# A hybrid encoder layer on one core: new order of the mixing's projections and jobs, gates as plain f32 products, W_out begun by halves, outputs transposed on TensorE

## The chip, the cores and the metric

One core of a Trainium2 chip runs the whole layer as one program. Its engines are TensorE (PE; its weight loads stand apart as PEld), VectorE (DVE), ScalarE (ACT), GpSimd (POOL) and SyncE (SP), which issues most transfers. The metric is the device time of one execution in microseconds, the median of several runs. Before: 1907.63 us, the median of 3 runs (1907.08 to 1908.33).

## The reference, cut to what matters

One layer on x of 256 tokens by 2048 features, all f32:

```python
x = x + 0.5 * swiglu(rms_norm(x, norm_ffn1), w1_ffn1, w3_ffn1, w2_ffn1)     # 2048 -> 5632 -> 2048
proj = rms_norm(x, norm_mix) @ w_in                                       # q 1024 | k 256 | v 256 | u 1024 | y 1024
q = apply_rope(rms_norm(q, q_norm), cos, sin); k = apply_rope(rms_norm(k, k_norm), cos, sin)
attn_out = bidir_gqa(q, k, v)                                             # 8 heads of 128, 2 for k and v
uc = centred_dw_conv(u, conv_w, conv_b)                                   # width 4
# rglru: r = sigmoid(blocks(uc) @ w_a + b_a); i = sigmoid(blocks(uc) @ w_i + b_i); log_a = -8 * softplus(-lam) * r
#        a = exp(log_a); h_t = a_t * h_(t-1) + sqrt(-expm1(2 * log_a)) * i * uc      (8 blocks of 128)
lru_out = (rglru(uc, ..., False) + rglru(uc, ..., True)) * gelu(y)
x = x + concatenate([attn_out, lru_out]) @ w_out
x = x + 0.5 * swiglu(rms_norm(x, norm_ffn2), w1_ffn2, w3_ffn2, w2_ffn2)
x = x + sigmoid(rms_norm(x, norm_ple) @ w_ple_gate) * (p @ w_ple_proj)
return rms_norm(x, norm_final)
```

## The kernel before, in words

The residual lies transposed in SBUF as `xs`: 128 features on the partitions, 16 blocks of features (`NKD`), 256 tokens. Every large product splits both operands in a rounded high part and a rest (`split`, lines 82 to 84: ACT casts the high part, DVE subtracts for the low part) and adds three products of the fp32r type.

A unit (`unit`, line 131) is one block of 128 output features: 1 MB of weights arrives in a raw buffer (3 of them, on SP's queue), is split in two halves of 8 blocks (4 buffers for each part), and each half gives 8 matmuls of 512 columns (high weights times both parts of the activations) and 8 of 256 (`unit_mms`, line 110). `total` (line 147) adds the two halves of the PSUM tile. The projections of q, k and v (`proj`, line 152) have the tokens on the partitions instead: 4 groups of weights, 24 matmuls of 512 columns each.

Four tiles of PSUM (`acc`) go to units, four (`trp`, tag "tr") to all else. The pool `mid` has 17 buffers of 4 KB per partition, `tok` has 4 of tag "tok", 4 of tag "att" and 6 of tag "tmp".

The mixing runs in this order: eight units of u in two groups, k and v, two groups of q, eight units of y in two groups, sixteen units of W_out. Beside it run jobs (Python generators); `tick` (line 97) advances each by one step, and is called once after each unit and after each group of weights of `proj`. `scan_job` (line 374) splits the convolved u and the gate weights (POOL subtracts), forms the gates with three matmuls each (`mm3`), the decays on ACT (sigmoid, exp, tanh, sqrt) with products on POOL, and runs the recurrence as DVE scans. `q_job` (line 527) does the attention of four heads; `y_job` (line 559) the gelu and its product with the sum of the scans. `rotate` (line 452) applies the rotary table with a scratch tile of tag "att", which the attention's `pt` and `pT_sb` use too. Each engine takes its instructions in one fixed order; a planner writes it when the program is built, by the order of writing as priority and by durations that it simulates.

The head (`lead`, line 251) begins three units with x and weights in pieces; the first pieces of x and the parameters go on ACT's queue. The end: the per-layer gate runs as units; the last two blocks of features are done by halves of the tokens (line 651); for each half the square sums are added by matmuls, the power -1/2 runs on POOL, a matmul broadcasts it over the partitions (`spread`, line 223), and `scale_out` (line 635) scales `xs` in place and stores it transposed; the host puts the axes right.

Of the kernel before, what the change touches and what calls it, by code (L numbers as in the profile page):

```python
# [38 lines left out]
WARM = 8  # L39
# [3 lines left out]
EARLY = 3  # L43
# [4 lines left out]
def hymba_layer(ctx, tc, xT, xrow, pT, w1a, w3a, w2a, win, wqkv, lruw, wout, w1b, w3b, w2b,  # L48
# [52 lines left out]

    def load(dst, src, eng=None):
        loads.append((eng or nc.sync).dma_start(dst, src))
# [27 lines left out]
    def unit(aT, srcs, nk, other=None):  # L131
# [12 lines left out]
        tick()  # L144
# [7 lines left out]
    def proj(aT, srcs):  # L152
        ps = [acc.tile([P, C], F32, tag="acc", name="acc") for _ in range(NH)]
        n = len(srcs)
        for g in range(n):
# [14 lines left out]
            tick()  # L170
# [13 lines left out]
    at = 0  # L184
    for n in PIECES[:EARLY]:
        load(flat(xs[:, at:at + n, :]), xT[:, at * S:(at + n) * S], nc.scalar)
        if at == 0:
            load(par_sb, par, nc.scalar)
        at += n
# [22 lines left out]
    def inv_rms(*ssq, halves=range(NH), keep=True):  # L212


        ps = trp.tile([P, 2, S], F32, tag="tr", name="sums")
        n = len(halves)
        for i, h in enumerate(halves):
            for j, s in enumerate(ssq):
                nc.tensor.matmul(ps[:, 0, i:i + 1], lhsT=s[:, h * P:(h + 1) * P], rhs=ones[:, 0:1],
                                 start=j == 0, stop=j == len(ssq) - 1)  # L220
        return spread(ps[:, 0, :n], n, keep)

    def spread(sums, n=NH, keep=True):

        r = sml.tile([P, NH], F32, tag="inv", name="inv", bufs=2)[:, :n]
        rsqrt(r, sums, D, n)
        dg = tmp("dg")
        pb = trp.tile([P, 2, S], F32, tag="tr", name="rows")
        for i in range(n):
            cols = slice(i * P, (i + 1) * P)  # L230
            nc.vector.tensor_scalar(dg[:, cols], ident, r[:, i:i + 1], None, op0=ALU.mult)
            nc.tensor.matmul(pb[:, 0, cols], lhsT=ones, rhs=dg[:, cols], start=True, stop=True)
        if not keep:
            return r, pb[:, 0, :n * P]
# [4 lines left out]
    def add_square(ssq, n, cols=slice(0, S), eng=None):  # L239

        if n == 0:
            nc.scalar.activation(ssq[:, cols], xs[:, n, cols], AF.Square)
            return
        t = tmp("sqr")[:, cols]
        nc.scalar.activation(t, xs[:, n, cols], AF.Square)  # L245
        (eng or nc.gpsimd).tensor_tensor(ssq[:, cols], ssq[:, cols], t, op=ALU.add)  # L246
# [127 lines left out]
    def scan_job(g, u):  # L374
        hi = mid.tile([P, 4, S], F32R, tag="mid", name="uc_hi")
        lo = mid.tile([P, 4, S], F32R, tag="mid", name="uc_lo")
        split(u, hi, lo, nc.gpsimd)
        raw = wraw.tile([P, 4, C], F32, tag="raw", name="raw")
        in_order(nc.sync.dma_start(flat(raw), lruw[g]), loads[-1])
        yield  # L380
        gw = []
        for d in range(2):
            wh = mid.tile([P, 2, C], F32R, tag="mid", name="gw_hi")
            wl = mid.tile([P, 2, C], F32R, tag="mid", name="gw_lo")
            split(raw[:, 2 * d:2 * d + 2, :], wh, wl, nc.gpsimd)
            gw.append((wh, wl))
        yield
        r, i, a = [], [], []
        for d in range(2):
            wh, wl = gw[d]  # L390
            for m in range(2):
                o = mtile("gate")
                for b in range(2):
                    ps = trp.tile([P, 2, S], F32, tag="tr", name="tr")
                    for j in range(2):
                        k = 2 * b + j
                        wc = slice(k * P, (k + 1) * P)
# [7 lines left out]
                yield  # L405
            cb = cneg[:, 8 * d + 4 * g:8 * d + 4 * g + 4].unsqueeze(2).broadcast_to([P, 4, S])
            nc.gpsimd.tensor_tensor(r[d], r[d], cb, op=ALU.mult)
        for d in range(2):
# [4 lines left out]
            nc.gpsimd.tensor_tensor(flat(i[d]), flat(i[d]), flat(u), op=ALU.mult)  # L413
        yield
# [3 lines left out]
        for d in range(2):  # L418
            nc.vector.scalar_tensor_tensor(flat(r[d]), flat(a[d]), 1.0, flat(r[d]),
                                           op0=ALU.add, op1=ALU.mult)  # L420
            nc.gpsimd.tensor_tensor(flat(r[d]), flat(r[d]), flat(i[d]), op=ALU.mult)
# [4 lines left out]
            yield  # L426
        nc.gpsimd.tensor_tensor(flat(i[0]), flat(i[0]), flat(i[1]), op=ALU.add)
# [3 lines left out]
    for g in range(2):  # L431
        u = mtile("uc")
        for k in range(4):
# [3 lines left out]
            nc.gpsimd.tensor_tensor(t, t, rmB, op=ALU.mult)  # L437
# [14 lines left out]
    def rotate(src, nh, half, m):  # L452
# [3 lines left out]
        sq = tok.tile([P, C], F32, tag="att", name="sq", bufs=ATT)[:, :w].rearrange("p (h d) -> p h d", d=HD)  # L456
# [61 lines left out]
    def values(qc, hp, pT2):  # L518
# [5 lines left out]
        dst = mix2[2 * qc + hp]  # L524
# [18 lines left out]
    mix2 = [mid.tile([P, 2, 2, S], F32R, tag="mid", name="mixT") for _ in range(NKD // 2)]  # L543
    mixT = [mix2[k // 2][:, k % 2, :, :] for k in range(NKD)]
# [14 lines left out]
    def y_job(g, y):  # L559
        for b in range(2):  # L560
            part = y[:, 2 * b:2 * b + 2, :]
            nc.scalar.activation(part, part, AF.Gelu_apprx_tanh)
            nc.vector.tensor_tensor(part, part, hsum[g][:, 2 * b:2 * b + 2, :], op=ALU.mult)
            dst = mix2[4 + 2 * g + b]
            split(part, dst[:, :, 0, :], dst[:, :, 1, :])
        yield

    for g in range(2):
        y = mtile("y")
        for k in range(4):  # L570
# [3 lines left out]
            nc.gpsimd.tensor_tensor(y[:, k, :], t, rmB, op=ALU.mult)  # L574
        jobs.append(y_job(g, y))

    tick()
# [184 lines left out]
```

## Time and profile before

| what | before |
|---|---|
| median of 3 runs | 1907.63 us |
| the profiled execution's own time | 1907.39 us |
| its span | 1905.6 us |
| PE busy | 1872.7 us (98%) |
| DVE busy | 1203.6 us (63%) |
| ACT busy | 965.2 us (51%) |
| POOL busy | 292.6 us (15%) |
| HBM read | 349.00 MB, 184 GB/s over the span |
| a load of 1024 KB of W_out, issue to landing (median) | 4.8 us |

A matmul's end is modelled, so a busy PE is not PE at its peak: the granted clock of a stretch says whether it ran at 2.4 GHz (1.00) or partly at 1.2 GHz. An engine's idle time is put down to what ended last before it went on. In the view by windows the busy times stand in the order PE, PEld, DVE, ACT, POOL, each with its count of instructions; in groups by line, the busy us, the mean ns of one and the idle us before them, with what ended it, stand behind the bar.

### The profile page before, as it was taken

What the parts mean: (1) busy time and instruction counts of PE and PEld (TensorE: products, weight loads), DVE (VectorE), ACT (ScalarE), POOL (GpSimd) and SP (SyncE); (2) the same over time, 40 slices, a digit from 0 to 9 for tenths busy, and PEclk for the clock granted to TensorE, in tenths of its full rate; (3) what the DMA queues carried; (4) which work ended last, traced back from release to release, by engine and by line L of the source; (5) the groups of instructions that cost most, each with busy time, mean ns of one, the idle gap of its engine ahead of it and who ended that gap; (6) DMA issues with size and microseconds to landing.
All of it is one profiled execution on the core that took longest, in us unless ns stands there. A gap on an engine that the chain in (4) does not pass through costs nothing.

```text
span 1905.6 us, 27228 instructions
## 1 busy us (share of the span) xinstructions
PE 1872.7 (98%) x10632; PEld 1640.3 (86%) x10632; DVE 1203.6 (63%) x1723; ACT 965.2 (51%) x1494; POOL 292.6 (15%) x225
## 2 busy tenths in 40 slices
PE   9999999999999999988999999999999999999997
PEld 7888888888888888867878888888888888888886
DVE  6766655556566556888767666655555666655686
ACT  6544444444444445677654544444444444555553
POOL 0111100011111001564211111110001111101143
PEclk9999999999999999999999999999999999999998
DMA  8555545655555556544345555555565555555552
GB/s 316 205 189 187 192 160 190 210 199 179 197 180 176 182 184 213 175 152 155 133 152 181 191 185 194 182 186 167 194 208 196 181 195 184 202 197 195 201 177 67
DMA packets 61552, 352.85 MB, mean 185 GB/s; under 512 B 6512, under 2 KB 12144, under 8 KB 31088
## 3 DMA queue, kind: packets, MB, share of 16 engines
q1 hardware_dynamic: 60848, 350.51, 54.0%
q8 instruction: 83, 1.36, 0.3%
q10 hardware_dynamic: 576, 0.61, 0.1%
q14 instruction: 45, 0.37, 0.1%
HBM read 349.00 MB, written 2.10 MB: 184 GB/s over the span
## 4 chain that ended last, share of the span: by engine, by line
PE 92%; DVE 3%; ACT 3%; issue 1%; POOL 1%; DMA 0%; SPq 0%; POOLq 0%; DVEq 0%; ACTq 0%
PE acc L115 59%; PE acc L117 30%; DVE wlo L84 1%; DVE gate L424 1%; DVE uc L370 0%; ACT whi L83 0%; PE po L522 0%; PE acc L656 0%; PE pe L115 0%; POOL us L437 0%; DMA xs<-in_xT 0%; PE tr L495 0%; ACT gate L403 0%; ACT a L410 0%; ACT L416 0%
## 5 line engine op out<-in xcount | busy, mean ns | idle before, releaser
L84 DVE TENSOR_TENSOR wlo<-raw,whi 128x1024 fp32r<-128x1024 f32 x722 | 806.5, 1126 | 594.7 <-ACT whi L83 577.5
L83 ACT CAST whi<-raw 128x1024 fp32r<-128x1024 f32 x722 | 687.0, 952 | 814.5 <-PE acc L115 553.9
L115 PE MATMUL acc<-aT,whi 128*128 128x512 f32 x3296 | 832.0, 393 | 1.2 <-DVE aT L88 1.2
L115 PEld LDWEIGHTS acc<-aT,whi 128*128 128x128 f32 x3296 | 593.1, 189 | 107.8 <-DVE aT L88 2.7
L117 PEld LDWEIGHTS acc<-aT,wlo 128*128 128x128 f32 x3296 | 451.4, 191 | 32.7
L117 PE MATMUL acc<-aT,wlo 128*128 128x256 f32 x3296 | 463.0, 283 | 0.0
L115 PE MATMUL acc<-hT,whi 128*128 128x512 f32 x1408 | 364.8, 392 | 0.0
L304 POOL TENSOR_TENSOR s<-s,rB 128x256 f32<-128x256 f32 x88 | 123.8, 1407 | 1067.7 <-ACT s L301 1061.9
L115 PEld LDWEIGHTS acc<-hT,whi 128*128 128x128 f32 x1408 | 247.6, 189 | 37.2
L117 PEld LDWEIGHTS acc<-hT,wlo 128*128 128x128 f32 x1408 | 202.7, 190 | 21.3
L117 PE MATMUL acc<-hT,wlo 128*128 128x256 f32 x1408 | 209.0, 282 | 0.0
L246 POOL TENSOR_TENSOR ssq<-ssq,sqr 128x256 f32<-128x256 f32 x58 | 54.4, 939 | 339.6 <-ACT sqr L245 339.6
L115 PE MATMUL acc<-mixT,whi 128*128 128x512 f32 x256 | 64.6, 393 | 1.4 <-DVE mixT L84 1.4
L115 PEld LDWEIGHTS acc<-mixT,whi 128*128 128x128 f32 x256 | 45.9, 189 | 10.2 <-DVE mixT L84 2.1
L315 DVE SCALAR_TENSOR_TENSOR xs<-acc,xs 128x256 f32<-128x256 f32 x128 | 53.3, 417 | 0.0
L87 ACT ACTIVATE aT<-xs,par_sb 128x256 fp32r<-128x256 f32 x64 | 31.5, 506 | 41.9 <-DVE xs L315 39.3
L92 PE MATMUL acc<-wlo,aT 128*128 128x512 f32 x96 | 40.4, 421 | 11.3 <-DVE wlo L84 11.3
L88 DVE SCALAR_TENSOR_TENSOR aT<-xs,par_sb,aT 128x256 fp32r<-128x256 f32 x64 | 38.2, 610 | 19.4 <-ACT aT L87 19.1
L306 DVE TENSOR_TENSOR u<-u,s 128x256 f32<-128x256 f32 x88 | 37.4, 426 | 9.1 <-DVE u L149 0.5
L93 PE MATMUL acc<-whi,aT 128*128 128x512 f32 x96 | 39.8, 415 | 0.0
L84 DVE TENSOR_TENSOR hT<-u,hT 128x256 fp32r<-128x256 f32 x88 | 38.0, 431 | 1.9 <-ACT hT L83 1.9
L300 DVE TENSOR_TENSOR z<-z,rB 128x256 f32<-128x256 f32 x88 | 37.4, 425 | 2.7
(168 smaller groups left out, 1001.5 us busy)
## 6 DMA issues: line engine op xcount, KB each, us to landing
raw<-in_w2a SPq DMA_DIRECT2D x64, 704.0 KB, 4.0
raw<-in_w1b SPq DMA_DIRECT2D x44, 1024.0 KB, 4.8
raw<-in_w3b SPq DMA_DIRECT2D x44, 1024.0 KB, 4.9
raw<-in_w2b SPq DMA_DIRECT2D x64, 704.0 KB, 4.0
raw<-in_w3a SPq DMA_DIRECT2D x43, 1024.0 KB, 4.8
raw<-in_w1a SPq DMA_DIRECT2D x42, 1024.0 KB, 4.8
raw<-in_win SPq DMA_DIRECT2D x16, 1024.0 KB, 4.9
raw<-in_wout SPq DMA_DIRECT2D x16, 1024.0 KB, 4.8
```

The source lines that it names most:

```text
L83: nc.scalar.copy(hi, src)
L84: (eng or nc.vector).tensor_tensor(lo, src, f32(hi), op=ALU.subtract)
L88: nc.vector.scalar_tensor_tensor(lo, src, gain, f32(hi), op0=ALU.mult, op1=ALU.subtract)
L92: nc.tensor.matmul(ps, lhsT=ah, rhs=wl, start=False, stop=False)
L93: nc.tensor.matmul(ps, lhsT=al, rhs=wh, start=False, stop=last)
L115: nc.tensor.matmul(ps, lhsT=ws[i][0], rhs=acts[i], start=first and i == 0, stop=False)
L117: nc.tensor.matmul(ps[:, 1, :], lhsT=ws[i][1], rhs=acts[i][:, 0, :], start=False, stop=last and i == n - 1)
L246: (eng or nc.gpsimd).tensor_tensor(ssq[:, cols], ssq[:, cols], t, op=ALU.add)
L300: nc.vector.tensor_tensor(z, z, rB, op=ALU.mult)
L304: nc.gpsimd.tensor_tensor(s, s, rB, op=ALU.mult)
L306: nc.vector.tensor_tensor(u, u, s, op=ALU.mult)
L315: nc.vector.scalar_tensor_tensor(xs[:, n, :], ps[:, j, :], 0.5, xs[:, n, :], op0=ALU.mult, op1=ALU.add)
```

## The change

Four parts.

- Mixing, order: k and v stand between the two groups of u; jobs advance after each half unit (after every second block of `proj`), and `scan_job` and `y_job` have shorter steps. Tiles for the mixed features are taken when they are written. The rows of W_out stand in a new order (`MIX_ORDER`), and its first two units are begun with the half that holds the first four heads and the first group of the recurrence.
- Mixing, work: the gates are one plain f32 matmul each, without splits; elementwise products on POOL go to DVE; `rotate` takes its scratch from tag "tok".
- The head: parameters and the third piece of x on SP's queue, ACT's table load ahead of its second piece, 6 warm-up matmuls for 8.
- The end: the gated features of both halves of the tokens first, then the blocks of `xs` are transposed on PE back to tokens on partitions, scaled from PSUM by a column on ACT or DVE into tiles of their own and stored in the final layout.

```diff
-WARM = 8
+MIX_ORDER = [*range(4), *range(8, 12), *range(4, 8), *range(12, 16)]
+WARM = 6
-EARLY = 3
+EARLY = 2
...
                 unit_mms(ps, part, aT[at:at + len(part)], at == 0, at + len(part) == n)
                 at += len(part)
-        tick()
+                tick()
...
-            tick()
+                if k % 2:
+                    tick()
...
+    load(par_sb, par)
+    load(flat(xs[:, 0:1, :]), xT[:, 0:S], nc.scalar)
     warm = sml.tile([P, 1], F32, tag="warm", name="warm", bufs=1)
     nc.gpsimd.memset(warm, 0.0)
     nc.scalar.activation(warm, warm, AF.Silu)
+    load(flat(xs[:, 1:2, :]), xT[:, S:2 * S], nc.scalar)
...
     def scan_job(g, u):
-        split(u, hi, lo, nc.gpsimd)
...
+            w = mid.tile([P, 2, C], F32, tag="mid", name="gw")
+            load(flat(w), lruw[g, :, 2 * C * d:2 * C * (d + 1)])
...
-                        mm3(ps[:, j, :], wh[:, m, wc], wl[:, m, wc], hi[:, k, :], lo[:, k, :],
-                            True, True)
+                        nc.tensor.matmul(ps[:, j, :], lhsT=gw[d][:, m, k * P:(k + 1) * P], rhs=u[:, k, :],
+                                         start=True, stop=True)
...
-            nc.gpsimd.tensor_tensor(r[d], r[d], cb, op=ALU.mult)
+            nc.vector.tensor_tensor(r[d], r[d], cb, op=ALU.mult)
+            yield
...
-            nc.gpsimd.tensor_tensor(flat(i[d]), flat(i[d]), flat(u), op=ALU.mult)
-        yield
+            nc.vector.tensor_tensor(flat(i[d]), flat(i[d]), flat(u), op=ALU.mult)
+            yield
...
-            nc.gpsimd.tensor_tensor(flat(r[d]), flat(r[d]), flat(i[d]), op=ALU.mult)
+            yield
+            nc.vector.tensor_tensor(flat(r[d]), flat(r[d]), flat(i[d]), op=ALU.mult)
+            yield
...
-        nc.gpsimd.tensor_tensor(flat(i[0]), flat(i[0]), flat(i[1]), op=ALU.add)
+        nc.vector.tensor_tensor(flat(i[0]), flat(i[0]), flat(i[1]), op=ALU.add)
...
-            nc.gpsimd.tensor_tensor(t, t, rmB, op=ALU.mult)
+            nc.vector.tensor_tensor(t, t, rmB, op=ALU.mult)
...
-        sq = tok.tile([P, C], F32, tag="att", name="sq", bufs=ATT)[:, :w].rearrange("p (h d) -> p h d", d=HD)
+        sq = tok.tile([P, C], F32, tag="tok", name="sq")[:, :w].rearrange("p (h d) -> p h d", d=HD)
...
-        nc.gpsimd.tensor_tensor(sv, sv, cb, op=ALU.mult)
+        nc.vector.tensor_tensor(sv, sv, cb, op=ALU.mult)
...
+    u_part(0)
     v_sb = const.tile([P, NH, 2 * HD], F32, name="v_sb")
     pkv = proj(am, [wqkv[2, k] for k in range(4)])
...
+    u_part(1)
     for qc in range(2):
         pq = proj(am, [wqkv[qc, k] for k in range(4)])
...
-            nc.gpsimd.tensor_tensor(y[:, k, :], t, rmB, op=ALU.mult)
-        jobs.append(y_job(g, y))
+            nc.vector.tensor_tensor(y[:, k, :], t, rmB, op=ALU.mult)
+            if k % 2:
+                jobs.append(y_job(g, k // 2, y[:, k - 1:k + 1, :]))
...
+    first = [acc.tile([P, 2, S], F32, tag="acc", name="acc") for _ in range(2)]
+    raws = []
+    for n in range(2):
+        raws.append(wraw.tile([P, 16, P], F32, tag="raw", name="raw"))
+        load(flat(raws[n]), wout[n, 0])
+    for j in (0, 8):
+        if j:
+            finish()
+        for n in range(2):
+            hi, lo = spl_pair()
+            split(raws[n][:, j:j + 8, :], hi, lo)
+            blocks = [mix2[k // 2][:, k % 2, :, :] for k in MIX_ORDER[j:j + 8]]
+            unit_mms(first[n], [(hi[:, i, :], lo[:, i, :]) for i in range(8)], blocks, j == 0, j == 8)
+            tick()
...
+    last_features(0)
+    last_features(1)
+    r0 = norms(0)
+    for b in range(4):
+        put(0, b, in_rows(0, b), r0)
+    ahead = [in_rows(1, b) for b in range(3)]
+    r1 = norms(1)
+    for b in range(3):
+        put(1, b, ahead[b], r1)
+    put(1, 3, in_rows(1, 3), r1)
```

`finish` advances the jobs until none is left. The new functions at the end:

```python
def last_features(h):          # the two last feature blocks for half h of the tokens
    ...
    nc.scalar.activation(last[i][:, cols], x, AF.Square)
    nc.scalar.activation(x, x, AF.Copy, scale=par_at(O_GF + n))
def norms(h):                  # three sum matmuls of one column, then the power on POOL
    ...
    rsqrt(r, ps[:, 0, :1], D, 1)
    return r
def in_rows(h, b):             # four blocks of features back to tokens on partitions
    ...
    for k in range(4):
        nc.tensor.transpose(ps[:, k * P:(k + 1) * P], xs[:, 4 * b + k, h * P:(h + 1) * P], ident)
    return ps
def put(h, b, ps, r):          # b odd: DVE, even: ACT
    if b % 2 == 0:
        outs[h, b // 2] = mid.tile([P, 2, C], F32, tag="mid", name="out")
    o = outs[h, b // 2][:, b % 2, :]
    if b % 2:
        nc.vector.tensor_scalar(o, ps, r, None, op0=ALU.mult)
    else:
        nc.scalar.activation(o, ps, AF.Copy, scale=r)
    eng = nc.scalar if (h, b) == (1, 2) else nc.sync
    eng.dma_start(out[h * P:(h + 1) * P, b * C:(b + 1) * C], o)
```

## Rows read from the trace of the kernel before

**Rows 1.** Windows: us; busy us (count) by engine; granted clock; DMA share; GB/s.

```profile
26.20:740.00 713.80, 713.80 (x4094) 628.32 (x4093) 429.85 (x628) 344.32 (x508) 71.91 (x58) 1.00 0.57 192
...
740.00:965.00 225.00, 207.19 (x1078) 175.64 (x1077) 172.11 (x213) 151.24 (x259) 91.88 (x51) 0.96 0.45 156
...
830.00:853.00 23.00, 17.32 (x58) 12.84 (x58) 22.47 (x23) 14.38 (x29) 13.83 (x8) 0.85 0.26 91
853.00:888.00 35.00, 27.65 (x117) 22.01 (x117) 27.21 (x31) 22.33 (x40) 15.63 (x8) 0.90 0.44 146
...
900.00:951.60 51.60, 51.60 (x299) 45.62 (x298) 37.36 (x62) 33.94 (x64) 9.98 (x9) 1.00 0.43 144
951.60:964.10 12.50, 7.90 (x31) 5.34 (x29) 6.62 (x17) 9.34 (x19) 0.72 (x1) 0.86 0.24 84
```

**Rows 2.** Waits of PE, 746.7 to 1050.8 us: total us, times, longest.

```profile
PE acc L92 <- DVE wlo L84: 11.3, 5, 4.7
```

**Rows 3.** DVE groups by line, 100 to 400 us, then 740 to 965 us.

```profile
L84 DVE TENSOR_TENSOR wlo<-raw,whi 128x1024 fp32r<-128x1024 f32 x96 | 117.6, 1225 | 122.9 <-ACT whi L83 122.8
...
L300 DVE TENSOR_TENSOR z<-z,rB 128x256 f32<-128x256 f32 x16 | 6.8, 426 | 0.5
...
L84 DVE TENSOR_TENSOR wlo<-raw,whi 128x1024 fp32r<-128x1024 f32 x60 | 87.0, 1464 | 23.0 <-ACT whi L83 18.9 <-ACT pT_sb L515 2.0 <-ACT rB L236 1.5
L424 DVE TENSOR_TENSOR_SCAN gate<-a,gate 128x256 f32<-128x256 f32 x16 | 18.3, 1199 | 0.0
```

**Rows 4.** Timeline of DVE and of POOL in the scan: start us, us.

```profile
810.61 9.80 DVE L84 TENSOR_TENSOR wlo<-raw,whi 128x1024 fp32r<-128x1024 f32 x3 [2.12 <-ACT whi L83]
...
832.14 6.74 DVE L424 TENSOR_TENSOR_SCAN gate<-a,gate 128x256 f32<-128x256 f32 x4
...
839.92 2.42 DVE L424 TENSOR_TENSOR_SCAN gate<-a,gate 128x256 f32<-128x256 f32 x4
...
815.94 3.39 POOL L413 TENSOR_TENSOR gate<-gate,uc 128x1024 f32<-128x1024 f32 x1
```

**Rows 5.** Timeline of PE in the mixing.

```profile
793.70 0.28 PE L91 MATMUL tr<-uc_hi,gw_hi 128*128 128x256 f32 x1
...
795.14 0.40 PE L91 MATMUL acc<-whi,aT 128*128 128x512 f32 x1
...
906.88 0.82 PE L513 MATMUL tr<-ident,pt 128*128 128x128 f32 x6
...
911.62 1.89 PE L522 MATMUL po<-pT_sb,v_sb 128*128 128x256 f32 x8
913.35 1.89 PE L495 MATMUL tr<-kT,qT 128*128 128x256 f32 x8
...
959.19 3.49 PE L522 MATMUL po<-pT_sb,v_sb 128*128 128x256 f32 x8 [0.95 <-ACT pT_sb L515]
...
972.62 2.00 PE L115 MATMUL acc<-mixT,whi 128*128 128x512 f32 x8
...
975.41 2.00 PE L115 MATMUL acc<-mixT,whi 128*128 128x512 f32 x8
```

**Rows 6.** Timeline of POOL, the rotation of the second group of q.

```profile
917.09 1.32 POOL L461 TENSOR_TENSOR qs<-qs,tabs 128x512 f32<-128x512 f32 x1 [17.41 <-DVE sq L460]
```

**Rows 7.** Timeline of the end: PE, POOL, DVE and SP's queue.

```profile
1889.99 0.84 PE L656 MATMUL acc<-aT,whi 128*128 128x256 f32 x5
...
1896.73 0.56 POOL L210 TENSOR_TENSOR inv<-rs_v,mhalf 128x1 f32<-128x1 f32 x1 [0.89 <-DVE rs_v L209]
...
1898.56 2.54 DVE L639 TENSOR_TENSOR xs<-xs,rows 128x256 f32<-128x256 f32 x5 [0.95 <-PE rows L232]
...
1899.00 2.93 SPq L641 DMA_DIRECT2D out<-xs  x5
```

**Rows 8.** The chain that ended last, in the head, and ACT's timeline there.

```profile
6.08 5.69 DMA xs<-in_xT
...
11.79 1.31 ACT L87 ACTIVATE aT<-xs,par_sb 128x256 fp32r<-128x256 f32 x3 [1.69 <-DMA xs<-in_xT]
```

More of the change, by code (lines that the diff above doesn't have):

```diff
@@ L100, in tick, with finish @@
                 jobs.remove(job)
+    def finish(done=lambda: not jobs):
+        while not done():
+            tick()
     def load(dst, src, eng=None):
@@ L556, in hymba_layer, with y_job @@
         jobs.append(q_job(qc, qro, qsc))
[L559 to L565, printed above, removed]
+    def y_job(g, b, part):
+        nc.scalar.activation(part, part, AF.Gelu_apprx_tanh)
+        nc.vector.tensor_tensor(part, part, hsum[g][:, 2 * b:2 * b + 2, :], op=ALU.mult)
+        dst = mix2[4 + 2 * g + b] = mixtile()
+        split(part, dst[:, :, 0, :], dst[:, :, 1, :])
         yield
     for g in range(2):
+        finish(lambda: hsum[g] is not None)
         y = mtile("y")
@@ L633, in hymba_layer @@
     last = [sml.tile([P, S], F32, tag=t, name="last", bufs=2) for t in ("ssq", "rB")]
-    def scale_out(h, rows, part, eng):
-        cols = slice(h * P, (h + 1) * P)
-        for at, n in ((0, 2), (2, 2)) if part == 0 else ((4, 4), (8, 4), (12, 4)):
-            o = xs[:, at:at + n, cols]
-            eng.tensor_tensor(o, o, rows.unsqueeze(1).broadcast_to([P, n, P]), op=ALU.mult)
-            b, e = at // 4, at % 4
-            nc.sync.dma_start(out[h, b, :, e:e + n, :], o)
     small = []
@@ L650, in hymba_layer @@
         small.append(t)
-    for h in range(NH):
+    def last_features(h):
         cols = slice(h * P, (h + 1) * P)
+        pss = []
         for i in range(2):
@@ L661, in hymba_layer @@
             nc.vector.tensor_tensor(g, g, rpB[:, cols], op=ALU.mult)
-            gated(n, g, pe[i], cols, nc.vector, last[i])
-        _, rf = inv_rms(ssq3, *last, halves=[h], keep=False)
-        if h == 0:
-            rows = tmp("rows")[:, :P]
-            nc.scalar.copy(rows, rf)
-            scale_out(0, rows, 0, nc.gpsimd)
-        else:
-            scale_out(0, rows, 1, nc.vector)
-            scale_out(1, rf, 0, nc.vector)
-            scale_out(1, rf, 1, nc.vector)
+            x = xs[:, n, cols]
+            nc.scalar.activation(g, g, AF.Sigmoid)
+            nc.vector.tensor_tensor(g, g, pe[i][:, cols], op=ALU.mult)
+            nc.vector.tensor_tensor(x, x, g, op=ALU.add)
+            nc.scalar.activation(last[i][:, cols], x, AF.Square)
+            nc.scalar.activation(x, x, AF.Copy, scale=par_at(O_GF + n))
+    def norms(h):
+        cols = slice(h * P, (h + 1) * P)
+        ps = trp.tile([P, 2, S], F32, tag="tr", name="sums")
+        for j, q in enumerate((ssq3, *last)):
+            nc.tensor.matmul(ps[:, 0, 0:1], lhsT=q[:, cols], rhs=ones[:, 0:1], start=j == 0, stop=j == 2)
+        r = sml.tile([P, NH], F32, tag="inv", name="inv", bufs=2)[:, :1]
+        rsqrt(r, ps[:, 0, :1], D, 1)
+        return r
+    def in_rows(h, b):
+        if b % 2:
+            ps = trp.tile([P, C], F32, tag="tr", name="out")
+        else:
+            ps = acc.tile([P, C], F32, tag="acc", name="out")
+        for k in range(4):
+            nc.tensor.transpose(ps[:, k * P:(k + 1) * P], xs[:, 4 * b + k, h * P:(h + 1) * P], ident)
+        return ps
+    outs = {}
+    def put(h, b, ps, r):
+        if b % 2 == 0:
+            outs[h, b // 2] = mid.tile([P, 2, C], F32, tag="mid", name="out")
+        o = outs[h, b // 2][:, b % 2, :]
+        if b % 2:
+            nc.vector.tensor_scalar(o, ps, r, None, op0=ALU.mult)
+        else:
+            nc.scalar.activation(o, ps, AF.Copy, scale=r)
[11 more added lines that the diff above has]
+    put(1, 3, in_rows(1, 3), r1)
 def _units(w, kc=None):
@@ L759 @@
     r = run_bass_kernel_spmd(nc, [sent], core_ids=[0])
[L760 to L761 removed]
+    return r.results[0]["out_0"].reshape(1, S, D)
```

95 lines of the change are left out of this document (37 added, 58 removed).

## The prediction

> **What bounds the kernel now.** I read the windows first, because TensorE (PE) is the bound and the question is where it is not full. Between 26.2 and 740 us PE is busy for the whole stretch at granted clock 1.00, so no edit outside the mixing, the head and the tail can gain [rows 1]. In the mixing three stretches fall short: 830 to 853 us (17.32 of 23.00 busy, clock 0.85), 853 to 888 us (27.65 of 35.00, 0.90) and 951.6 to 964.1 us (7.90 of 12.50, 0.86). Idle: 5.68 + 7.35 + 4.60 = 17.6 us. Clock, as (1 - granted) times the stretch: 3.45 + 3.50 + 1.75 = 8.7 us. Together 26.3 us can be had back in the mixing, and no more.
>
> Next, the waits of PE: the largest, 11.3 us in 5 pieces, is a matmul of a projection waiting for the low part of a weight split by VectorE (DVE) [rows 2]. So in the first two stretches DVE is late; its window says so too, 22.47 busy of 23.00 [rows 1]. Why is it late? By lines, one 128x1024 split takes 1225 ns on DVE between 100 and 400 us, but 1464 on the mean of 60 in the mixing [rows 3]. The timeline shows when: three splits take 9.80 us from 810.61 while GpSimd (POOL) runs products of the scan, one of them 3.39 us from 815.94; four scans take 6.74 us from 832.14 and the like four 2.42 us, 0.605 each, from 839.92 [rows 4]. Taking every form between 740 and 965 us at its short executions removes 42 us from DVE (an estimate; the splits give 60 x 0.24 = 14 of it, the scans 16 x 0.59 = 9.5). DVE was busy 172 us there [rows 1]; undisturbed it would be 130.
>
> **Part by part. Mixing: work moved.** Seven kinds of products go from POOL to DVE: 14 of 128x1024 (the decay constant 4, input times u 4, the product after the root 4, the sum of both directions 2), 16 of 128x256 for u and y, 4 of 128x512 and 2 of 128x256 in the rotation. At 1.225 and 0.426 us [rows 3], and 0.7 for 128x512 (an estimate between these two), that is 17.2 + 7.7 + 2.8 = 27.7 us. The splits of u (2 of 128x1024) and of the gate weights (4) vanish from POOL, with as many casts on ScalarE (ACT), 6 us off the latter. DVE then has 130 + 28 = 158 us where it had 172, and POOL keeps only small powers.
>
> This rests on the long executions standing only beside POOL [rows 4]; were they caused by something that stays, DVE would have 172 + 28 = 200 us, the first rival. The Trainium skill ("SBUF — State Buffer", Who interferes with whom) gives a mechanism: DVE's second read port is shared with GpSimd under an exclusive lock, so a DVE operation with two SBUF inputs waits out a GpSimd one that reads SBUF. By that rule DVE has the 158 us; the trace agrees with it in the two groups of four scans, 6.74 and 2.42 us.
>
> **Mixing: gates as plain f32 products.** 32 products of two instructions each replace 96 matmuls. Twelve of the old take 1.44 us (793.70 to 795.14), 0.12 each: 11.5 us. Eight f32 instructions of the same size in the values take 1.73 us (911.62 to 913.35), 0.216 each: 64 are 13.8 us [rows 5]. PE pays 2.3 us, in full since it is the bound.
>
> **Mixing: order.** k and v now come between the two groups of u, and jobs advance every half unit. I counted DVE against PE by section at undisturbed durations. Second u group: per unit two splits 2.45, total and product 0.85, three taps 1.3 (estimate from the 0.426), so 18.4 for four; k's norm and rotation 4.1 (an estimate, some 16 small steps); five scan products 6.1; 29 us of DVE in 24 of PE (four units of 5.59 and eight f32 gate instructions). First y group: 13.2 own, 4.9 rotation, 8 attention (estimate: half of the 16 us of its lines now), 8.5 scan (8 x 0.605 + 3 x 1.225), 1.4 gelu; 36 us in 31 of PE (four units and 9 of attention). In the other five sections DVE has slack of 3 to 15 us. Overload: 5 + 5 = 10 us. Four buffers of split weights are four half units of 2.79 us (972.62 to 975.41), 11 us of PE [rows 5], and hide all of it if they are full when the overload starts. If nothing hides it, PE waits 10 us and loses clock in the proportion seen before (8.7 on 17.6): 15 us. I take the middle, 7.5: the stretch from 740 then lasts 208.5 us after the terms below, and DVE is busy 158 of it, 76%, the same share as now (172 of 225), so the forecast asks no better packing of DVE than there is.
>
> **Mixing: rotation and W_out.** Before, the rotation of the second q waits for scratch held by the attention: POOL stands 17.41 us until 917.09 [rows 6], and the last attention job ends PE's third gap. With scratch from the other pool this goes, and the first halves of two output units (2 x 2.79 = 5.6 us) need none of the late tiles. What is late next is the last gelu: seven steps on ACT and DVE of 0.4 to 0.7 us each and perhaps a table load, about the 5.6 us of cover, so 0 to 1 us shows; it is inside the 7.5. Two raw weights held there leave one buffer for the next load, which is issued about 11 us (four half units) ahead of need.
>
> Mixing: 26.3 - 7.5 - 2.3 = 16.5 us gained.
>
> **Tail.** PE's last product before ends at 1890.8, with sums put between; without these about 1890.3 [rows 7]. Before, the power on POOL (0.56 us, at 1896.73), a broadcast and five scalings (2.54 us from 1898.56) follow, and the second half's five issues begin at 1899.00. After: 6 sum matmuls (0.1 us each, an estimate from the 0.12 of the gates), 16 transposes of the first half and 12 of the second, 6 sums, the power and its step on DVE (1.0), then outputs from PSUM in pairs, one on ACT and one on DVE, 0.7 each. Six transposes took 0.82 us at 906.88 [rows 5], so 28 are 3.8. From 1890.3: sums to 1890.9, transposes to 1894.7, sums to 1895.3, power to 1896.3, first output at 1897.0, so the issues begin 2.0 us sooner. The 1 MB behind them then needed the rest of the span, 6.6 us from 1899.0, and still does, since it was issued over 2.93 us and now over little less. The separate output tiles keep a scaling from waiting for a transfer; I cost that at nothing. Bounds: 0 if the first half's scalings get in front of the last sigmoid chain (four of 0.7 us on two engines, and hops), 5 if the sums go ahead of the transposes and the issues shrink to 1 us. I take 2.
>
> **Head.** The parameters and the third piece of x move from ACT's queue to SP's, two issues in front of the later pieces and weights; the table load comes before the second piece; two warm-up matmuls go. PE is fed by the fourth piece of x, for which ACT waits 1.69 us at 11.79; its transfer is 5.69 us of the chain, from the issue at 6.08 [rows 8], so the queue was full of bytes, and the bytes in front are the same. Bounds: -0.5 (first split sooner) to +1.5 (third piece late). I take +0.5.
>
> **Sum.** The profiled execution took 1907.4 (span 1905.6 and 1.8 around it; the median of the runs is 0.2 above). 1907.4 - 16.5 - 2 + 0.5 = 1889.4, say 1889. Its own range: best 26.3 - 2.3 + 5 + 0.5 = 29.5 less, 1878; worst 26.3 - 15 - 2.3 + 0 - 1.5 = 7.5 less, 1900.
>
> **Rivals.**
> 1. The stretching stays. DVE then has 200 us; at an occupancy between its mean (0.765) and its fullest stretch (0.977), 0.87, that is 230 us for what lasts 225: 1907.4 + 5 - 2 + 0.5 = 1911. For it: I infer the cause from overlaps in time. Against: the two groups of four scans, and the splits in the first 700 us, where POOL is seldom busy. Chance 0.05.
> 2. The transposes of the tail run at 1.2 GHz. Eight f32 instructions took 3.49 us at 959.19, in the stretch of clock 0.86, against 1.89 at 911.62 [rows 1, 5], 1.85 times; 28 transposes cost 3.2 us more and the tail loses 1.2: 1892.6. For it: transposes stand alone there for 3 us. Against: PE comes straight from matmuls, and six at 906.88 ran at full speed, though among matmuls. The Trainium skill ("TensorE: Matmul & The Clock Gate", Part 4: PE-mode transpose) says that the full clock does not engage for transposes; no row here shows a stretch of them alone. Chance 0.13.
> 3. The change doesn't do what it says: the planner sets each engine's order by its own simulated times, and could put the late halves of the output units first, so that the third gap (4.60 + 1.75 = 6.3 us) stays: 1895.7. Against: the early halves are written first and need nothing late. Chance 0.08.
> 4. Slower: DVE becomes the bound with holes in it. The scan chain now alternates ACT and DVE on a queue that is taken in order; each hop that the planner mistimes leaves DVE idle with the splits queued behind, and PE behind these. The place is the second u and the first y group. It decides at 158 / 225 = 70% occupancy: below that the mixing is longer than now. Between the 53% of 951.6 to 964.1 and the mean of 76.5% [rows 1] lies 65%: 243 us, 18 more: 1907.4 + 18 - 2 + 0.5 = 1924. For it: both groups are over 100% by count. Against: 900 to 951.6, where DVE and ACT alternate most, had 72% without making PE wait. Chance 0.18.
>
> **Chances.** Forecast 0.56. A measurement of this kernel can tell about 0.2%, 3.8 us: below 1903.8 is faster, above 1911.4 slower. Faster: 0.56 + 0.13 + 0.08 + 0.01 (the lower edge of rival 4), 0.78. Slower: 0.02 of rival 1 and 0.13 of rival 4, 0.15. The same: 0.03 + 0.04, 0.07. The range goes from 1878 to 1908: below it lies 0.03, above 0.03 of rival 1 and 0.14 of rival 4.
>
> **What would show it.** Splits in the mixing near 1225 ns on the mean, and scans near 2.4 us for four: else rival 1. PE idle under 8 us between 746 and 964, with no half clock: else rival 4, and the wait on the low split then stands in the two overloaded sections. No gap before W_out's first full units: else rival 3. Transposes of the tail 0.1 to 0.14 us apart: else rival 2, or the tail's order. The first real matmul by 5 us and no PE gap over 1 us at 12: else the head. Wrong altogether if the gates on PE cost far over 13.8 us, or PE waits for ACT's tables instead.

## The result, and the profile after

The changed kernel takes 1884.24 us (median of 4 runs, 1883.70 to 1884.46), the kernel before 1907.98 (4 runs, 1907.08 to 1908.74): a ratio of 0.9875 with a 95% interval of 0.9858 to 0.9892, or 23.7 us less. Forecast were 1889 us and "faster" at 0.78.

The profiled execution of the changed kernel took 1884.04 us with a span of 1882.2. Four points of the two traces split the difference of the spans, 23.4 us. The mixing runs from the first matmul of its projections to the first one of the second FFN; the tail from the first product for the last two blocks of features to the end of the span.

| stage | before, us | after, us | gained | forecast |
|---|---|---|---|---|
| head and first FFN, to the mixing's start | 746.7 | 749.1 | -2.4 | -0.5 |
| mixing | 304.1 | 282.3 | 21.8 | 16.5 |
| second FFN and gate | 827.9 | 827.9 | 0 | 0 |
| tail | 26.9 | 22.9 | 4.0 | 2 |

The page's first and fourth part, busy time and the shares of the chain that ended last by engine:

```profile
span 1882.2 us, 27165 instructions
...
PE 1868.5 (99%) x10626; PEld 1639.5 (87%) x10626; DVE 1182.6 (63%) x1745; ACT 960.3 (51%) x1496; POOL 209.0 (11%) x181
...
PE 97%; ACT 1%; DVE 1%; DMA 0%; issue 0%; SPq 0%; DVEq 0%; POOLq 0%; POOL 0%; ACTq 0%
```

Windows of the changed kernel: the head, PE's time on the second group of u, the two stretches of the mixing that had been short of PE in [rows 1], PE's time on the first group of y, the stretch that now holds all that is left of its idle time, and two of the end (columns as in [rows 1]):

```profile
0.00:26.20 26.20, 21.61 (x88) 16.26 (x89) 16.14 (x36) 16.79 (x38) 0.92 (x9) 0.93 0.86 307
799.35:824.07 24.72, 24.72 (x142) 21.70 (x141) 19.41 (x35) 18.84 (x35) 2.46 (x2) 1.00 0.52 174
830.00:853.00 23.00, 23.00 (x103) 18.95 (x102) 22.66 (x32) 14.73 (x24) 0.00 (x0) 1.00 0.53 183
853.00:888.00 35.00, 35.00 (x172) 29.66 (x171) 26.03 (x44) 26.91 (x67) 4.82 (x4) 1.00 0.46 153
877.56:909.00 31.44, 31.44 (x183) 27.77 (x182) 27.90 (x48) 29.61 (x55) 2.63 (x2) 1.00 0.35 118
...
900.00:975.00 75.00, 72.43 (x414) 63.11 (x413) 59.02 (x93) 47.80 (x80) 3.79 (x4) 1.00 0.48 164
...
1871.00:1876.40 5.40, 4.63 (x43) 4.43 (x43) 3.28 (x11) 2.86 (x8) 1.12 (x2) 1.00 0.28 105
1876.40:1882.20 5.80, 0.00 (x0) 0.00 (x0) 1.33 (x2) 1.19 (x2) 0.00 (x0) 0.76 0.71 264
```

From 830 to 888 us PE is full at granted clock 1.00, where it had been busy for 17.32 of 23 and 27.65 of 35 us at 0.85 and 0.90. DVE is still busy for 22.66 of 23: it is packed, not freed. All waits of PE in the mixing, 749 to 1031 us (total, times, longest), answer to [rows 2]; the wait on a weight's low part is gone:

```profile
PE acc L123 <- DVE mixT L88: 2.0, 1, 2.0
PE po L522 <- ACT pT_sb L515: 0.4, 1, 0.4
PE tr L513 <- DVE pt L506: 0.2, 1, 0.2
```

DVE by lines in the mixing, splits of a weight and scans, answering to [rows 3] (their means were 1464 and 1199 ns; over the same 740 to 965 us as there, the splits' mean is 1221 ns too):

```profile
L88 DVE TENSOR_TENSOR wlo<-raw,whi 128x1024 fp32r<-128x1024 f32 x89 | 108.4, 1221 | 41.5 <-ACT whi L87 39.6 <-ACT rB L239 1.5
...
L421 DVE TENSOR_TENSOR_SCAN gate<-a,gate 128x256 f32<-128x256 f32 x16 | 9.8, 671 | 0.0
```

DVE's timeline, answering to [rows 4 and 6]: both groups of four scans at the short duration, a rotation's product that was POOL's, and the last two splits that PE waits for:

```profile
835.17 2.43 DVE L421 TENSOR_TENSOR_SCAN gate<-a,gate 128x256 f32<-128x256 f32 x4
...
838.63 2.43 DVE L421 TENSOR_TENSOR_SCAN gate<-a,gate 128x256 f32<-128x256 f32 x4
...
857.32 0.69 DVE L460 TENSOR_TENSOR qs<-qs,tabs 128x512 f32<-128x512 f32 x1
...
943.39 0.69 DVE L88 TENSOR_TENSOR mixT<-po,mixT 128x512 fp32r<-128x512 f32 x1 [3.59 <-ACT mixT L87]
944.00 0.68 DVE L88 TENSOR_TENSOR mixT<-y,mixT 128x512 fp32r<-128x512 f32 x1
```

PE's timeline, answering to [rows 5]: gates in plain f32 and the products after them, a longer stretch of such gates, then the last gap of the mixing:

```profile
798.67 1.02 PE L392 MATMUL tr<-uc,gw 128*128 128x256 f32 x4
799.35 2.20 PE L123 MATMUL acc<-aT,whi 128*128 128x512 f32 x8
801.39 1.11 PE L125 MATMUL acc<-aT,wlo 128*128 128x256 f32 x8
...
849.61 1.89 PE L392 MATMUL tr<-uc,gw 128*128 128x256 f32 x8
...
940.74 1.99 PE L522 MATMUL po<-pT_sb,v_sb 128*128 128x256 f32 x8 [0.40 <-ACT pT_sb L515]
944.74 0.73 PE L123 MATMUL acc<-mixT,whi 128*128 128x512 f32 x2 [2.00 <-DVE mixT L88]
```

ACT's timeline at that gap:

```profile
942.77 0.59 ACT L87 CAST mixT<-po 128x512 fp32r<-128x512 f32 x1 [1.60 <-PE po L522]
943.25 0.62 ACT L87 CAST mixT<-y 128x512 fp32r<-128x512 f32 x1
```

The timeline of all engines at the end, answering to [rows 7], with a few of its lines:

```profile
1871.18 1.18 PE L695 MATMUL out<-ident,xs 128*128 128x128 f32 x9
...
1872.34 2.27 PE L695 MATMUL out<-ident,xs 128*128 128x128 f32 x19
...
1874.06 4.28 SPq L709 DMA_DIRECT2D out<-out  x7
...
1874.50 0.31 ACT L676 ACTIVATE last<-xs 128x128 f32<-128x128 f32 x1
...
1876.32 1.41 DVE L705 TENSOR_SCALAR out<-out,inv 128x512 f32<-128x512 f32 x2 [0.67 <-POOL inv L216]
```

And ACT's and PE's timelines in the head, answering to [rows 8]:

```profile
12.63 1.71 ACT L91 ACTIVATE aT<-xs,par_sb 128x256 fp32r<-128x256 f32 x4 [0.78 <-DMA xs<-in_xT]
```

```profile
13.71 0.50 PE L123 MATMUL acc<-aT,whi 128*128 128x512 f32 x1 [2.49 <-DVE aT L92]
```

### The profile page after: what moved, and what is told of

Its sections match the earlier page's. It is cut to its first block, busy times and chain, and to the rows that moved or that the text cites. A ratio compares the mean times of both kernels' runs of the same rounds, so it can differ in the third digit from the quotient of the medians.

```text
span 1882.2 us, 27165 instructions
## 1 busy us (share of the span) xinstructions
PE 1868.5 (99%) x10626; PEld 1639.5 (87%) x10626; DVE 1182.6 (63%) x1745; ACT 960.3 (51%) x1496; POOL 209.0 (11%) x181
## 4 chain that ended last, share of the span: by engine, by line
PE 97%; ACT 1%; DVE 1%; DMA 0%; issue 0%; SPq 0%; DVEq 0%; POOLq 0%; POOL 0%; ACTq 0%
PE acc L123 60%; PE acc L125 31%; PE acc L97 1%; PE acc L95 1%; PE acc L96 1%; PE tr L392 1%; DMA xs<-in_xT 0%; PE acc L664 0%; PE pe L123 0%; PE po L522 0%; DVE wlo L88 0%; ACT whi L87 0%; PE small L653 0%; PE pe L125 0%; PE tr L495 0%
## 5 line engine op out<-in xcount | busy, mean ns | idle before, releaser
L88 DVE TENSOR_TENSOR wlo<-raw,whi 128x1024 fp32r<-128x1024 f32 x722 | 792.5, 1105 | 597.7 <-ACT whi L87 583.1
L304 ACT ACTIVATE s<-z 128x256 f32<-128x256 f32 x88 | 36.4, 413 | 4.3 <-DVE z L303 4.3
```

What stands on the lines that cost most here:

```text
L88: (eng or nc.vector).tensor_tensor(lo, src, f32(hi), op=ALU.subtract)
L304: silu = nc.scalar.activation(s, z, AF.Silu)
```

## The experiments

"Mixing", "start" and "tail" below are the stages of the table, read from each run's trace in the same way; times are medians of 4 runs (t1: 11; d1: one); the brackets hold the ratio to the kernel before on the same chip and its 95% interval. A trace is of one execution, which need not lie at the median: those of p1 (1890.0 us) and p2 (1894.8) lie 2.9 and 1.9 us below it, those of r1 (1888.8) and k1 (1893.9) 2.3 and 1.5 us above.

**The head of before in the changed kernel** (h1). The edit puts the order and the queues of the first loads and the warm-up count back:

```diff
-WARM = 6
+WARM = 8
-EARLY = 2
+EARLY = 3
-    load(par_sb, par)
-    load(flat(xs[:, 0:1, :]), xT[:, 0:S], nc.scalar)
+    at = 0
+    for n in PIECES[:EARLY]:
+        load(flat(xs[:, at:at + n, :]), xT[:, at * S:(at + n) * S], nc.scalar)
+        if at == 0:
+            load(par_sb, par, nc.scalar)
+        at += n
...
-    load(flat(xs[:, 1:2, :]), xT[:, S:2 * S], nc.scalar)
```

> The changed kernel with the head of before (parameters and third piece of x on ACT's queue, 8 warm-up matmuls). Theory (the new head costs what the first mixing matmul came later, 749.11 against 746.72): 2.4 us less than the changed kernel, about 1881.8, and the mixing starts at 746.7. Rival (the head only shifts with the phase of the clock from run to run): no steady difference, 1884.

1882.93 us (0.9868, 0.9854 to 0.9881); start 747.4, 1.7 us sooner than 749.1 where 2.4 was expected; mixing 282.3, tail 22.9, both unchanged. Its window of the head:

```profile
0.00:26.20 26.20, 22.98 (x100) 16.95 (x101) 16.69 (x37) 17.65 (x38) 0.92 (x9) 1.00 0.88 317
```

The granted clock stays at 1.00, where the changed head has 0.93, a stretch of 3.4 us at the lower level from 15.7 us. PE's wait before the fourth piece of x is 1.48 us here and 2.49 there.

**The products of POOL on DVE, alone in the kernel before** (p1), seven lines of this form:

```diff
-            nc.gpsimd.tensor_tensor(r[d], r[d], cb, op=ALU.mult)
+            nc.vector.tensor_tensor(r[d], r[d], cb, op=ALU.mult)
```

> The kernel before with one part: the seven kinds of products of the mixing on DVE instead of POOL; the splits of u and of the gate weights stay on POOL, order and everything else as before. Theory (POOL beside DVE stretches DVE and makes PE wait): the waits of PE on low splits fall from 11.3 us to under 4, mean split in the mixing under 1.30 us, 10 to 17 us less, 1891 to 1898; the third gap (951.6 to 964.1) stays. Rival (the new order is what helps, and DVE only gets more work): 1905 or above.

1892.87 us (0.9917, 0.9904 to 0.9931). By the medians it is 15.7 us less than before. In the traced execution the mixing takes 286.6 us, 17.5 less than before; splits have a mean of 1244 ns over the mixing (1386 before, over the same stretch); DVE, with all these products added, is busy for 223.9 us of the mixing instead of 228.7. PE's waits there, the longest kinds:

```profile
PE tr L513 <- DVE pt L506: 3.2, 3, 1.9
PE acc L92 <- DVE wlo L84: 2.1, 2, 1.3
```

The wait on the low part of a weight goes from 11.3 us [rows 2] to 2.1 with this edit alone.

**The reverse: the changed kernel with those products back on POOL** (p2; the same lines the other way).

> The changed kernel with the seven kinds of products back on POOL, all else as changed. Theory of the stretching: splits in the mixing at 1.35 us or more on the mean, PE waits again 8 us or more plus half clock, 1892 to 1902. Rival (order, gates and scratch carry the gain): within 3 us of 1884.

1896.77 us (0.9942, 0.9927 to 0.9957). Mixing 294.5, 12.2 longer than in the changed kernel; two stretches at half clock, 10.2 us together, return, splits have a mean of 1310 ns instead of 1221, under the 1350 or more that were expected, and PE's idle time is 10.9 us instead of 2.6. PE's two largest waits:

```profile
PE tr L513 <- DVE pt L506: 4.8, 1, 4.8
PE acc L96 <- DVE wlo L88: 2.3, 1, 2.3
```

By the medians the move is worth 15.7 us when made first and 12.5 when made last (1884.24 against 1896.77); in the traced mixings it is 17.5 and 12.2, and the other edits are worth 9.6 alone and 4.3 on top of it. The two overlap; that they shorten the same waits is the likely reason.

**Useless work on POOL beside the first FFN** (d1). The changed kernel, with 32 products of 128x1024 and then 32 fills of the same size on POOL that nothing reads; all else is computed as before:

```diff
...
+                        if part == 0:
+                            nc.gpsimd.tensor_tensor(jk, jk, jk, op=ALU.mult)
+                        else:
+                            nc.gpsimd.memset(jk, 0.0)
```

> The changed kernel with useless work on POOL in the first feed-forward layer, where PE never waits: in its first half 32 products of 128x1024 that read SBUF, in its second 32 fills of the same size that only write. Theory (DVE's operation with two SBUF inputs waits while POOL reads): splits beside the products 1.4 us or more on the mean against 1.22, beside the fills 1.22 to 1.25. Rival (POOL's writes or its mere activity stretch DVE): both stretched alike. PE hides either, so the mixing starts where it did.

The planner let POOL begin at once: products from 2.5 to 128 us, fills until 164. DVE's splits beside the products (26 to 128 us), then beside the fills (130 to 165 us), and POOL's own groups:

```profile
L88 DVE TENSOR_TENSOR wlo<-raw,whi 128x1024 fp32r<-128x1024 f32 x28 | 46.9, 1688 | 1.8 <-ACT whi L87 1.8
...
L88 DVE TENSOR_TENSOR wlo<-raw,whi 128x1024 fp32r<-128x1024 f32 x15 | 18.5, 1230 | 4.6 <-ACT whi L87 4.6
```

```profile
L314 POOL TENSOR_TENSOR jk<-jk 128x1024 f32<-128x1024 f32 x32 | 69.5, 2173 | 1.9
L316 POOL MEMSET jk<- 128x1024 f32 x32 | 30.6, 955 | 1.6
```

The same split in the same stretch of the changed kernel takes 1223 ns on the mean of 39. Beside fills, which write as much and read nothing, a split stays at 1230 ns; beside products the mean is 465 ns more. It mixes two kinds: 16 of the 28 splits had none of the added products beside them and took 1.21 to 1.23 us, the 12 that had one took 1.21 to 2.92 us, 2.32 on the mean. That PE would hide either was wrong: the mixing begins 21 us later (770.1), and is as long as ever (282.3); the single run took 1905.18 us. Between 26 and 130 us PE, which has no idle time there in the changed kernel, is idle for 8.7 us and loses 5.1 to half clock; the rest of the 21 us lies in the head, where the products stood beside the first splits. The longest of PE's waits for a low part:

```profile
92.64 2.08 PE L125 MATMUL acc<-aT,wlo 128*128 128x256 f32 x8 [4.56 <-DVE wlo L88]
```

**The gates in plain f32 on top of p1** (g1):

```diff
-                        mm3(ps[:, j, :], wh[:, m, wc], wl[:, m, wc], hi[:, k, :], lo[:, k, :],
-                            True, True)
+                        nc.tensor.matmul(ps[:, j, :], lhsT=gw[d][:, m, wc], rhs=u[:, k, :],
+                                         start=True, stop=True)
```

> The kernel before with products on DVE (1892.9, mixing 286.6 us) and also plain f32 gates, so no splits of u and gate weights; order, scratch, W_out and the end as before. Theory from the changed trace (four f32 instructions in 0.68 us, 64 are 10.9, against 11.5): 0.6 us less on PE, and 12.1 + 4.8 us of POOL and 6 of ACT go, so 0.6 to 2 us less than products on DVE alone. Rival (my prediction's price of 13.8): 2.3 us more.

1892.40 us (0.9921, 0.9905 to 0.9938) against 1892.87 for p1: no difference that these runs can tell. Mixing 289.4 us against 286.6, PE's idle time 6.6 against 6.9, half clock 6.8 us long instead of 3.4. Without idle time and clock the mixing's work on PE is some 1.4 us longer, so these gates gain nothing on PE. DVE is busy for 212.9 us of the mixing, 11 less than in p1: what left POOL here are its six splits of 128x1024, and the weight splits on DVE are back at 1221 ns.

**The gates in eight stretches of four products instead of sixteen of two** (v1, with the head of h1):

```diff
-                    yield
                 (r, i)[m].append(o)
+                yield
+                yield
```

> The head of before, and the gates of the recurrence formed in 8 stretches of four products instead of 16 of two, all else as changed. Theory (each change from an f32 stretch back to a unit costs PE about 0.2 us: eight matmuls of 512 columns after one take 2.20 us, otherwise 2.00): mixing 1.6 us shorter than 282.3, 1881.3 against 1882.9 with the old head alone. Rival (longer steps hold up ACT and DVE, or PSUM tiles): mixing 282 or more.

1882.89 us (0.9872, 0.9856 to 0.9889), the same as h1's 1882.93; mixing 281.96, 0.35 less than in the changed kernel; the expected 1.6 was too much. On PE the planner's order has 11 stretches of gates here and 15 in the changed kernel, not 8 and 16.

**k and v after both groups of u** (k1), in the changed kernel:

```diff
     u_part(0)
+    u_part(1)
     v_sb = const.tile([P, NH, 2 * HD], F32, name="v_sb")
...
-    u_part(1)
```

> The changed kernel with both groups of u first and then k and v, all else as changed. Theory (k and v between the groups give DVE slack between two sections that each want 85 to 120% of it): PE waits for splits return, 3 to 8 us, 1887 to 1892. Rival (buffers of split weights hide it, as they do in the changed kernel): within 1.5 us of 1884.

1892.33 us (0.9924, 0.9909 to 0.9938); by the medians 8.1 us more than the changed kernel, just over what was expected; the traced mixing takes 292.5, 10.2 longer, of which 6.8 are idle time of PE and 1.7 half clock. Splits keep their 1220 ns, but DVE is late again in one place. Its window there, and PE's largest wait in the mixing:

```profile
830.00:875.00 45.00, 40.12 (x173) 31.24 (x172) 39.66 (x57) 36.23 (x65) 3.62 (x3) 1.00 0.43 144
```

```profile
PE acc L96 <- DVE wlo L88: 4.4, 5, 1.7
```

**The rotation's scratch back among the attention's tiles** (r1):

```diff
-        sq = tok.tile([P, C], F32, tag="tok", name="sq")[:, :w].rearrange("p (h d) -> p h d", d=HD)
+        sq = tok.tile([P, C], F32, tag="att", name="sq", bufs=ATT)[:, :w].rearrange("p (h d) -> p h d", d=HD)
```

> The changed kernel with the rotation's scratch again in the attention's tag, all else as changed (mixing 282.3 us, median 1884.2). Theory (the scratch held up the second q): the rotation waits 10 us or more, the mixing is 3 to 7 us longer, 1887 to 1891. Rival (in the new order the attention has let go of its tiles by then): under 1 us.

1886.53 us (0.9895, 0.988 to 0.9909); by the medians 2.3 us more than the changed kernel, a little less than expected. The traced mixing takes 286.4, 4.1 longer: 2.0 us more of idle time and one stretch of 3.4 us at half clock (1.7 us) make 3.7 of it. DVE begins the second rotation of q 27.6 us later than in the changed kernel. Its line here, and then there:

```profile
907.20 1.43 DVE L459 TENSOR_TENSOR sq<-qs,tabs 128x256 f32<-128x256 f32 x4
```

```profile
879.62 0.76 DVE L459 TENSOR_TENSOR sq<-qs,tabs 128x256 f32<-128x256 f32 x2
```

**No halves for W_out's first two units** (w1): `first` and its loops go, all sixteen units are whole.

```diff
-        ps = first[n] if n < 2 else unit(order, [wout[n, 0]], NKD)
+        ps = unit(order, [wout[n, 0]], NKD)
```

> The changed kernel with W_out's units whole from the first, rows in the same new order, all else as changed. Theory (the two first halves cover the last tiles): PE waits 2.0 us for a mixed tile now and 4 to 7.6 us without the cover, the mixing is 2 to 5.6 us longer, 1886 to 1890. Rival (the planner fills the place with the same halves, as it already reorders): under 1 us.

1884.58 us (0.9881, 0.9867 to 0.9896); mixing 282.39, waits of PE the same three, 2.0, 0.4 and 0.2 us. The planner interleaves the first two units by itself: in this kernel too PE does the 12 products of 512 columns whose tiles are there (937.42 to 940.6 us) before the last six transposes of the attention. The halves as written are worth nothing here.

**The new end alone in the kernel before** (t1: all edits from `last_features` on).

```diff
-    for h in range(NH):
+    def last_features(h):
...
-            scale_out(1, rf, 1, nc.vector)
+    put(1, 3, in_rows(1, 3), r1)
```

> The kernel before with the end of the changed one (outputs transposed on PE, scaled from PSUM into own tiles), all else as before. Theory: 4.0 us less than before, 1903.9, since from the first low product of the last two blocks to the end it took 26.9 us before and 22.9 after. Rival (the end gained because PE reached it in another state): under 2 us.

1905.22 us against 1908.52 (0.9982, 0.9973 to 0.9991), 3.3 less. The tail takes 23.0 us, 3.9 less; the profiled execution lost 2.1 of them at the start (748.8), with a stretch at half clock from 14.7 us although the head is that of before.

**Two more warm-up matmuls in the changed head** (h2), and **the changed kernel once more** (a1), on one chip:

```diff
-WARM = 6
+WARM = 8
```

> The changed kernel with 8 warm-up matmuls for 6, the rest of the new head kept. Theory (PE's clock falls at 14 to 19 us because PE waits 2.5 us for the fourth piece of x, which the new queue brings 0.8 us later): no change, mixing starts at 748 to 750 with 3.4 us of half clock. Rival (the shorter warm-up is why): no half clock behind 11 us, 1.7 us less.

> The changed kernel once more, beside the three that follow. 1884.2 us; start of the mixing between 747.5 and 750 us, mixing 282.3 us, end 22.9 us.

h2: 1883.93 us (0.9876, 0.9862 to 0.9891), start 747.7 with no half clock in the head, mixing 283.9 with a stretch of 3.4 us at half clock behind its last gap (from 944.2 us). a1: 1884.12 (0.9877, 0.9863 to 0.9892), start 748.8, half clock from 14.6 us, mixing 282.3. Medians within 0.2 us: the clock stays up in this execution's head, what that gives is lost again behind the gap, and the time does not show it. Nor is it shown that the warm-ups kept it up: in p2, with six, it stayed up too, and in t1, with eight, it fell.

h1 and v1 have the lowest medians of this case, but the gain on the changed kernel is not beyond these runs' noise: v1 and a1 ran on one chip, 1882.89 against 1884.12, 1.2 us apart with ranges that touch (1882.35 to 1883.46, 1883.24 to 1884.78).

## Why the prediction was right, and where it missed

**The bound and its cause.** Right, and shown. PE waited for DVE because DVE's instructions with two inputs in SBUF stretch beside POOL's that read SBUF. p1 takes most of the POOL work away and with it four fifths of the wait; p2 brings the stretching back, with waits of 10.9 us; d1 puts such work where there was none. That fills leave a split alone says that it is not POOL being busy; that it is the reading, and not something else that a product does and a fill does not, is the simplest account of it. The Trainium skill ("SBUF — State Buffer", Who interferes with whom) states just this difference, between a GpSimd instruction that reads and one that only writes; 1688 against 1230 ns agrees. Forecast was that DVE's busy time falls by 14 us in spite of 28 us of added products; over the mixing it fell from 228.7 to 212.8 us, by 15.9. The moved products alone gave 4.8 of it (223.9 in p1), and the other 11 came when POOL's own splits for the gates went too (212.9 in g1). Rival 1 (the stretching stays) fell with the means of 1221 ns and 2.43 us for four scans.

**The overload by section.** My count named two sections where DVE has more to do than PE, 29 us in 24 and 36 in 31. Neither came as counted: DVE is busy for 19.41 of 24.72 us of the second u group and for 27.90 of 31.44 of the first y group. Its fullest stretch, 22.66 of 23 us, lies behind the first of them: while PE is on the first group of q, DVE still has products of the second u group, and the first scans. Work runs on into the next section, and my count kept it in its own. PE never waits for the split of a weight; whether the four buffers of split weights or the slack of the next section hide the rest is not shown. I gave 7.5 us for what would not be hidden; all waits of the mixing are 2.6 us, without any half clock. This is the term that was mis-sized most, 4.9 us of the 5.3 by which the mixing did better. What I left out of that sum is that the order itself decides: with k and v after both groups of u the same instructions, as short, make the kernel 8.1 us slower by the medians, 10.2 in the traced mixing (k1). It lay within my bound of 15 us, so rival 4 (DVE late, with PE behind it) had a real place, at about half of its price of 18 us. The chosen order does without it.

**The gates.** Forecast +2.3 us of PE. The mixing without idle time and clock is 304.1 - 17.8 - 8.5 = 277.8 us before and 282.3 - 2.6 = 279.7 after: +1.9, if nothing else changed on PE; g1 against p1 gives +1.4. My price of one f32 instruction, 0.216 us, was right: a stretch of four takes 1.02 us (798.67) and one of eight 1.89 (849.61), 0.217 for each further one. Start to start the four seem cheaper (0.68 us to the next product, 0.17 each), and v1 and g1 expected their gains from that. But the product behind them is on the record as begun at 799.35, before the last of the four has ended at 799.69, and what the four lack there the eight products behind them have too much (2.04 us, start to start, and not 1.84). So there is no loss per change from f32 to other products that fewer stretches could save, and v1 saved next to none. Why the sum came out at 1.9 or 1.4 and not 2.3 is open.

**Rotation and W_out.** The rotation's wait for scratch was real: 2.3 us by the medians and 4.1 in the traced mixing (r1), against the 6.3 us that I counted for the whole third gap. That the first halves of two output units "need none of the late tiles" failed: PE does 12 of their 16 products of 512 columns and then waits for the tile of the other four. Nor do the halves change anything (w1), since the planner takes the early products first in either form. So rival 3 had the planner's freedom right and its direction wrong. "What is late next is the last gelu" failed too. The last gap, 2.00 us at 944.74, ends with the split of a y tile whose gelu product was done at 918.5 us; its cast stands on ACT behind the cast of the last attention job's values, which waits 1.60 us for PE. What is late is the attention, with the y tile behind it in ACT's order.

**Tail.** Forecast 2 us, measured 4.0 (t1 alone: 3.9). From the tail's start, the second half's first issue came at 20.3 us before (1899.00 - 1878.7) and comes at 17.7 now (its first scalings end near 1877.0, from 1859.3): 2.6 us, where I had 2.0. The step that failed is that the 1 MB behind them needed "the rest of the span, 6.6 us from 1899.0, and still does": it needs 5.2 us now. Its four issues end by 1878.3, 1.3 us after they begin, where five took 2.93 us. Both my bounds held. Rival 2 fell: 28 transposes stand 0.11 us apart from 1871.2 to 1874.6, at granted clock 1.00, and the clock falls from 1879.4 only, after PE's work is done. The Trainium skill ("TensorE: Matmul & The Clock Gate", Part 4: PE-mode transpose) says that the full clock does not engage for transposes; the measurement decides, in this place, right behind 8 us of matmuls at granted clock 1.00, and what transposes do to the clock elsewhere no run here shows. One thing was as I had feared for the lower bound: the last block's square sum on ACT starts at 1874.50, behind two scalings of the first half that began at 1873.35, though its input was there at 1873.2.

**Head.** Forecast +0.5 with an upper bound of 1.5; measured +2.4 in this execution, and the claim "no PE gap over 1 us at 12" failed with 2.49 us. The fourth piece of x landed at 12.6 us, against 11.8 in the kernel before and 12.2 with the old head in the changed kernel (h1). That "the bytes in front are the same" was not enough is plain; that the two loads put on SP's queue in front of this piece are why is likely and not shown, since h1 issues it at the same time, 6.43 us against 6.41. The rest is clock: a stretch of 3.4 us at the lower level (1.7 us of time) follows the wait in five of the six profiled executions with the changed head and six warm-ups (d1, disturbed there, left out), and in one of six with the head of before. Over these twelve the start is at 749.0 and 747.5 us on the mean: 1.5 us is the head's price, part transfer, part clock.

**Sum.** 21.8 + 4.0 - 2.4 = 23.4 us of span, for the forecast 16.5 + 2 - 0.5 = 18: right in sign and mechanism, and the time 4.8 us below the forecast. The tail gained 2.0 us more than forecast and the head lost 1.9 more; that these two cancel is luck.

## What to carry to other kernels

Before a bound engine is relieved by moving work to POOL, look whether both read SBUF: here 28 us of products moved to DVE left it 5 us less busy, and 16 with POOL's splits gone too, because its other instructions went back to their short durations. Count the bound engine's helper by section, and let what does not fit run on into the next one: the same instructions in an order that puts the two groups of u side by side cost 8 us. Read the price of an instruction from stretches of different length, not from one start to the next across a change of kind. A planner that reorders can make an edit of the written order worthless; compare the order that it emits before crediting the edit.

## What the runs showed of the hardware

- POOL's products pay too: one of 128x1024 takes 2173 ns on the mean beside DVE's splits (d1), and 1.97 us in a stretch of four; a fill of that size takes 955 ns. DVE's smallest steps, 128x16, go from 0.17 us to 1.65 beside such a product, and one with a single tile and a constant as inputs to 1.86. A split that overlaps a product is not always the one that is longer: two of the twelve that had one of d1's products beside them kept 1.21 us.
- Plain f32 instructions of 128x256 come 0.217 us apart at granted clock 1.00 (1.02 us for four, 1.89 for eight). A product right behind them is on the record as begun 0.34 us before the last of them has ended.
- In the head, the granted clock fell to its lower level behind a wait of PE of 2.3 to 3.0 us in six executions (five with the changed head, and t1 with that of before). It stayed up in six where the longest wait was 0.6 to 2.1 us (p2 with the changed head, the others with that of before), and behind 2.55 us in h2. t1 and h2 have the same wait and eight warm-ups both; what tells these two apart is open.
